# The last four experts' gate and up products: two parts of the tokens side by side, weight splits behind the sums, final-norm steps behind the product

## The chip, the cores and the metric

The kernel runs on one core of one Trainium2 chip. The metric is the device time of one execution in microseconds (us); the median over runs is what counts. The core's engines run side by side, each through a queue of its own in program order: TensorE (PE) does matrix products into the accumulation memory PSUM, ScalarE (ACT) and VectorE (DVE) work on elements, GpSimd (POOL) does small arithmetic and issues the indirect DMAs and some direct ones, SyncE (SP) issues the other DMAs. An instruction starts when its queue has reached it and all that it waits for has signalled.

## The reference

One encoder layer over 2048 tokens of width 1024. What the change touches is its last part, a mixture of 16 experts in which each expert picks its 256 tokens, and the norm at the very end:

```python
def expert_choice_moe(h, w_router, w_gate, w_up, w_down):
    ...
    gates, idx = lax.top_k(aff.swapaxes(1, 2), cap)
    xin = jax.vmap(lambda hb, ib: hb[ib])(h, idx)
    a = jnp.einsum("becd,edf->becf", xin, w_gate)
    b = jnp.einsum("becd,edf->becf", xin, w_up)
    y = jnp.einsum("becf,efd->becd", jax.nn.silu(a) * b, w_down)
    y = y * gates.astype(y.dtype)[..., None]
    out = jax.vmap(lambda ib, yb: jnp.zeros((S, D), yb.dtype).at[ib].add(yb))(
        idx.reshape(B, -1), y.reshape(B, -1, D))
    return out
...
    x = x + expert_choice_moe(rms_norm(x, g_ffn[l]), ...)
    return rms_norm(x, g_final)
```

All of it is float32. The kernel keeps that precision by splitting every operand into a high part, which TensorE takes exactly, and the rest: a = ah + al, and a product is ah·bh + ah·bl + al·bh.

## The kernel before, in words

`phase_moe` loops over the experts x = 0 to 15. An expert's 256 tokens lie transposed in `ht` (128 partitions, 8 blocks of the width, two parts, 256 tokens: part 0 the high one, part 1 the rest). Its weights are fetched in 12 jobs of 1 MB (job 12x + 2c + g: gate, g = 0, and up, g = 1, of the column blocks c = 0 to 3; then four jobs of the down matrix). `prep(i)` (L1721) splits job i: ACT copies the raw tile `wr` into `wh` (L1725), DVE subtracts to give `wl` (L1726), and then `fetch(i + 3)` puts the next load on SP's queue. Raw tiles have three buffers, split ones four.

For a column block c, PE multiplies the gate columns into PSUM tiles named `pa`, the up columns into tiles named `pb`, each in two halves j of 128 columns. Each of the names `pa`, `pb`, `py` and `tr` has two PSUM buffers that are taken in turn, so a new tile waits until the last but one of its name has been read.

Experts 0 to 11 and the last four (x at or above `LATE` = 12) do this in two ways:

- **Experts 0 to 11** (L1861 to L1866): for each half j a tile of its own holds two sums side by side. One product with 512 columns multiplies `wh` by both parts of the tokens (L1863), one with 256 columns multiplies `wl` by the high part (L1864). ACT copies the second sum out (L1865), DVE adds the first (L1866); after the gate's two halves ACT applies SiLU in place (L1869).
- **Experts 12 to 15** (L1856 to L1859): both halves in one tile, three products with 256 columns each (`mm3`, L45 to L47) that add up in PSUM. After both gate and up, ACT applies SiLU out of PSUM (L1883) and DVE multiplies by the up tile in PSUM (L1886).

Then `split` (L35) writes the product's high part `ah` (ACT, L37) and the rest `al` (DVE, L38). After the four blocks comes the down product (`mm3` again): two sums of 512 columns by two token halves, the first into `py`, the second into one `pa` and one `pb` tile. So an expert takes nine `pa` tiles in the first way (eight and one), five in the second (four and one).

In the last four experts the final norm is done alongside. `late_rows` gathers the residual rows of the expert's tokens; `late_piece` (L1774) adds the gated down product to them (L1777, DVE, reading PSUM; this is what sets the tile free), squares them on ACT (L1779) and multiplies by the norm's gain (L1780). All other rows are normed in sixteen blocks t of 128 rows by `final_step(n)` (L1791), which a fixed list `at` spreads over steps n = 12(x − 12) + job: `final_load(t)` at n = at[t] (POOL queue, L1742), `final_rows` two steps later (ACT squares, L1749, then a chain of 14 small POOL instructions, L1732, L55 and three times L67 to L70, that gives the reciprocal root), `final_scale` at +4 (DVE, L1755), `final_store` at +5 (SP, L1758). At its step 16 the rows of the expert before are normed (`late_norm`, L1788 and L1789), at 17 scattered to the output by two indirect DMAs (L1761). Before, even steps of the column blocks stand behind the gate's products, odd ones at the end of the block; in the down product there is one after each job.

Nothing reorders this: the schedule is manual, so the queues hold the instructions in the order in which the Python text issues them.

Of the kernel before, what the change touches and what calls it, by code (L numbers as in the profile page):

```python
# [10 lines left out]
F = mybir.dt.float32  # L11
# [4 lines left out]
AF = mybir.ActivationFunctionType  # L16
# [4 lines left out]
S, D, P = 2048, 1024, 128  # L21
# [22 lines left out]
def mm3(nc, ps, lh, ll, rh, rl, start, stop, **kw):  # L44
    nc.tensor.matmul(ps, lh, rh, start=start, stop=False, **kw)  # L45
    nc.tensor.matmul(ps, lh, rl, start=False, stop=False, **kw)  # L46
    nc.tensor.matmul(ps, ll, rh, start=False, stop=stop, **kw)  # L47
# [1586 lines left out]
def phase_moe(e):  # L1634


    nc, tc = e.nc, e.tc
    E, C = 16, 256
    LATE = E - 4
    with ExitStack() as ctx:  # L1640
# [194 lines left out]
        for x in range(E):  # L1835
# [8 lines left out]
            for c in range(4):  # L1844
                pp = []
                for g in range(2):
                    i = 12 * x + 2 * c + g
                    if c < 3 or g == 0:
                        prep(i + 3)
                    wh, wl = W.pop(i)  # L1850
                    s = gp.tile([P, 2, C], F, name=("si", "up")[g]) if x < LATE else None
                    if x >= LATE:
                        p = ps.tile([P, 2, C], F, name=("pa", "pb")[g])
                    for j in range(2):
                        js = slice(j * P, j * P + P)
                        if x >= LATE:  # L1856
                            for k in range(8):
                                mm3(nc, p[:, j], wh[:, k, js], wl[:, k, js], ht[:, k, 0], ht[:, k, 1], k == 0, k == 7)
                            continue  # L1859

                        p = ps.tile([P, 2, C], F, name=("pa", "pb")[g])  # L1861
                        for k in range(8):
                            nc.tensor.matmul(p, wh[:, k, js], ht[:, k], start=k == 0, stop=False, skip_group_check=True)  # L1863
                            nc.tensor.matmul(p[:, 0], wl[:, k, js], ht[:, k, 0], start=False, stop=k == 7, skip_group_check=True)  # L1864
                        nc.scalar.activation(s[:, j], p[:, 1], AF.Copy)  # L1865
                        nc.vector.tensor_add(s[:, j], s[:, j], p[:, 0])  # L1866
                    pp.append(s if x < LATE else p)
                    if g == 0 and x < LATE:
                        nc.scalar.activation(s, s, AF.Silu)  # L1869
                    if g == 0:  # L1870
                        final_step(i - 12 * LATE)
                if c == 0 and x + 1 < E:
                    lists(x + 1)
                if c == 1:
                    onehots(x + 2)
                    if x >= LATE:
                        late_rows(x)
                if c == 2 and x + 1 < E:
                    turn(x + 1, 0, 0)
                    turn(x + 1, 0, 1)  # L1880
                if x >= LATE:
                    s = gp.tile([P, 2, C], F, name="si")
                    nc.scalar.activation(s, pp[0], AF.Silu)  # L1883
                else:
                    s = pp[0]
                nc.vector.tensor_mul(s, s, pp[1])  # L1886
                split(nc, ah[:, 2 * c:2 * c + 2], al[:, 2 * c:2 * c + 2], s)
                if c == 3:
                    prep(12 * x + 10)
                elif c == 0 and x + 1 == E:  # L1890
                    fetch(len(jobs) - 1)
                final_step(12 * x + 2 * c + 1 - 12 * LATE)
            if x + 1 < E:
                ys = YS[x] = [gp.tile([P, D], F, name="y", bufs=2) for _ in range(2)]
            else:
# [215 lines left out]
```

## Time and profile before

| | us |
|---|---|
| median of three runs | 3091.11 (3089.67 to 3092.14) |
| the profiled execution, by its own time | 3091.91 |
| span of its records, first to last instruction | 3090.0 |
| mean granted TensorE clock over the span | 0.984 of full |
| PE busy | 2982.7 (97%) |
| DVE busy | 2034.8 (66%) |
| ACT busy | 1625.9 (53%) |
| POOL busy | 951.8 (31%) |

The last four experts run from 2797 us on. How to read it: an engine's busy share says little by itself; what counts is which engine is never idle in a stage, and what would make it wait. The timeline view lists an engine's instructions with the idle time ahead of each and the releaser in brackets; the windows view gives busy times, granted clock and DMA share of a stretch.

### The profile page before, as it was taken

The page shows a single profiled execution, that of the slowest core. Times are in us where ns is not written, and L with a number is a line of the kernel's source. Part 1 is how long each engine was busy: PE and PEld are TensorE (multiplying, and loading weights), DVE is VectorE, ACT ScalarE, POOL GpSimd, SP SyncE. Part 2 cuts the span into 40 slices and gives each one's busy share as a digit, 9 for nine tenths or more (in the row PEclk, how much of TensorE's full clock was granted, in tenths as well). Part 3 has the DMA queues.
Part 4 walks back from the last instruction along what each step waited for, and adds up shares of the span by engine and source line. Part 5 has one row for each costly group of instructions (what it writes and reads, how often), then busy time and mean ns, then how long its engine had stood idle before and what let it go on. Part 6 is the DMA issues. An engine that isn't in the chain of part 4 may idle for free.

```text
span 3090.0 us, 44235 instructions
## 1 busy us (share of the span) xinstructions
PE 2982.7 (97%) x16408; PEld 2501.3 (81%) x16409; DVE 2034.8 (66%) x3697; ACT 1625.9 (53%) x2744; POOL 951.8 (31%) x942
## 2 busy tenths in 40 slices
PE   7999999899999999999999998799999999999998
PEld 7997767677777777789788886588888888889998
DVE  5557878787878787665444445766666666666765
ACT  4444796576666667115433333455555555554544
POOL 1223568676845555101000001000000000003564
PEclk8999999999999999999999999899999999999999
DMA  5766163032121211456111112476777766668885
GB/s 190 223 207 186 40 190 80 17 77 65 32 77 48 65 42 52 147 198 204 46 55 62 63 55 97 146 218 204 219 220 213 224 216 205 205 205 259 300 297 208
DMA packets 314505, 452.35 MB, mean 146 GB/s; under 512 B 21185, under 2 KB 230337, under 8 KB 312946
## 3 DMA queue, kind: packets, MB, share of 16 engines
q1 hardware_dynamic: 282792, 373.08, 38.6%
q0 software_dynamic: 14928, 54.34, 6.1%
q10 hardware_dynamic: 16570, 22.11, 2.2%
q8 instruction: 129, 2.11, 0.3%
q14 instruction: 86, 0.70, 0.1%
HBM read 361.06 MB, written 88.28 MB: 145 GB/s over the span
## 4 chain that ended last, share of the span: by engine, by line
PE 87%; DVE 4%; ACT 2%; POOL 2%; DMA 2%; issue 2%; ACTq 0%; SPq 0%; POOLq 0%; DVEq 0%
PE po L922 7%; PE pa L1863 5%; PE pb L1863 5%; PE pst L889 3%; PE pmax L837 3%; PE pst L891 3%; PE pst L890 3%; PE pb L1864 3%; PE pa L1864 3%; PE po L924 2%; PE co L45 2%; PE co L47 2%; PE co L46 2%; PE pa L45 2%; PE pa L47 2%; PE pa L46 2%
## 5 line engine op out<-in xcount | busy, mean ns | idle before, releaser
L1726 DVE TENSOR_TENSOR wl<-wr,wh 128x2048 fp32r<-128x2048 f32 x191 | 436.2, 2291 | 285.0 <-ACT wh L1725 283.8
L894 ACT ACTIVATE ph<-pst 128x512 fp32r<-128x512 f32 x512 | 305.2, 596 | 232.8 <-PE pst L891 220.7
L906 DVE TENSOR_TENSOR pl<-pst,ph 128x512 fp32r<-128x512 f32 x512 | 351.2, 686 | 79.3 <-ACT pst L895 74.5
L838 DVE TENSOR_REDUCE mt<-pmax 128x1 f32<-128x512 f32 x496 | 338.6, 684 | 68.9 <-PE pmax L837 67.1
L1725 ACT ACTIVATE wh<-wr 128x2048 fp32r<-128x2048 f32 x191 | 362.2, 1905 | 36.2 <-PE pb L47 22.6
L895 ACT ACTIVATE pst<-pst 128x512 f32<-128x512 f32 x512 | 304.4, 595 | 0.0
L903 POOL TENSOR_SCALAR part<-ph,va 128x512 f32<-128x512 f32 x160 | 253.3, 1583 | 98.7 <-ACT ph L894 87.7
L1863 PE MATMUL pa<-ht,wh 128*128 128x512 f32 x768 | 274.5, 400 | 2.7 <-DVE si L1866 1.9
L1863 PE MATMUL pb<-ht,wh 128*128 128x512 f32 x768 | 272.2, 397 | 0.0
L1761 POOL DMA_INDIRECT x_s<-y,idx x24 | 46.3, 1929 | 717.1 <-ACT y L1924 621.1
L837 PE MATMUL pmax<-kh,q 96*128 96x512 f32 x496 | 200.6, 406 | 17.6 <-DVE mt L838 12.9
L1864 PE MATMUL pb<-ht,wl 128*128 128x256 f32 x768 | 215.5, 281 | 0.0
L1864 PE MATMUL pa<-ht,wl 128*128 128x256 f32 x768 | 215.5, 281 | 0.0
L905 POOL TENSOR_TENSOR acc<-acc,part 128x512 fp32r<-128x512 f32 x160 | 208.1, 1300 | 13.4
L889 PE MATMUL pst<-q,kl 96*128 96x512 f32 x512 | 207.3, 405 | 1.2 <-DVE pl L906 1.2
L922 PE MATMUL po<-ph,va 128*128 128x512 f32 x512 | 203.9, 398 | 0.0
L891 PE MATMUL pst<-q,kh 97*128 97x512 f32 x512 | 203.6, 398 | 0.2 <-ACT q L847 0.2
L922 PE MATMUL po<-pl,va 128*128 128x512 f32 x512 | 202.6, 396 | 0.1
L890 PE MATMUL pst<-q,kh 96*128 96x512 f32 x512 | 202.5, 396 | 0.0
L1863 PEld LDWEIGHTS pa<-ht,wh 128*128 128x128 f32 x768 | 144.2, 188 | 37.0 <-DVE si L1866 2.4
L1863 PEld LDWEIGHTS pb<-ht,wh 128*128 128x128 f32 x768 | 144.1, 188 | 34.9
L1864 PEld LDWEIGHTS pa<-ht,wl 128*128 128x128 f32 x768 | 145.1, 189 | 0.4
(659 smaller groups left out, 7971.5 us busy)
## 6 DMA issues: line engine op xcount, KB each, us to landing
wr<-in_w_exp_gate SPq DMA_DIRECT2D x64, 1024.0 KB
wr<-in_w_exp_up SPq DMA_DIRECT2D x64, 1024.0 KB
wr<-in_w_exp_down SPq DMA_DIRECT2D x63, 1024.0 KB
xr<-in_xT SPq DMA_DIRECT2D x16, 512.0 KB
wr<-in_x SPq DMA_DIRECT2D x16, 512.0 KB
k_s<-put SPq DMA_DIRECT2D x16, 512.0 KB
q<-q_s SPq DMA_DIRECT2D x32, 256.0 KB
wt<-in_xf SPq DMA_DIRECT2D x32, 256.0 KB
```

Of the source, the lines that this page charges most:

```text
L838: nc.vector.tensor_reduce(mt[:, t, j:j + 1], p, axis=AX.X, op=OP.max)
L889: nc.tensor.matmul(p, kl[:, ks], qh[0:96], start=True, stop=False)
L890: nc.tensor.matmul(p, kh[0:96, ks], ql, start=False, stop=False)
L891: nc.tensor.matmul(p, kh[:, ks], qh, start=False, stop=True)
L894: nc.scalar.activation(ph, p, AF.Exp, scale=scale)
L895: nc.scalar.activation(p, p, AF.Exp, scale=scale)
L906: return ph, pl, lambda: nc.vector.tensor_sub(pl, p, ph.bitcast(F))
L922: nc.tensor.matmul(OT[h, c], v[:, 0:128], t, start=kt == 0 and i == 0, stop=False, skip_group_check=True)
L1725: nc.scalar.activation(W[i][0], r, AF.Copy)
L1726: eng.tensor_sub(W[i][1], r, W[i][0].bitcast(F))
L1863: nc.tensor.matmul(p, wh[:, k, js], ht[:, k], start=k == 0, stop=False, skip_group_check=True)
L1864: nc.tensor.matmul(p[:, 0], wl[:, k, js], ht[:, k, 0], start=False, stop=k == 7, skip_group_check=True)
```

## The change

Experts 12 to 15 now make gate and up as the others do: two products for each block of the width instead of three, two tiles, ACT copies, DVE additions, SiLU in place. In them `prep(i + 3)` is called behind the two halves' sums (and the SiLU) instead of ahead of the products. And both final-norm steps of a column block are called at its end, behind the product, the split and, in block 3, `prep`; those in the down product stay where they were. The experts 0 to 11 are left as they are.

```diff
--- before.py
+++ after.py
@@ -1845,18 +1845,13 @@
                 pp = []
                 for g in range(2):
                     i = 12 * x + 2 * c + g
-                    if c < 3 or g == 0:
+                    more = c < 3 or g == 0
+                    if more and x < LATE:
                         prep(i + 3)
                     wh, wl = W.pop(i)
-                    s = gp.tile([P, 2, C], F, name=("si", "up")[g]) if x < LATE else None
-                    if x >= LATE:
-                        p = ps.tile([P, 2, C], F, name=("pa", "pb")[g])
+                    s = gp.tile([P, 2, C], F, name=("si", "up")[g])
                     for j in range(2):
                         js = slice(j * P, j * P + P)
-                        if x >= LATE:
-                            for k in range(8):
-                                mm3(nc, p[:, j], wh[:, k, js], wl[:, k, js], ht[:, k, 0], ht[:, k, 1], k == 0, k == 7)
-                            continue
 
                         p = ps.tile([P, 2, C], F, name=("pa", "pb")[g])
                         for k in range(8):
@@ -1864,10 +1859,13 @@
                             nc.tensor.matmul(p[:, 0], wl[:, k, js], ht[:, k, 0], start=False, stop=k == 7, skip_group_check=True)
                         nc.scalar.activation(s[:, j], p[:, 1], AF.Copy)
                         nc.vector.tensor_add(s[:, j], s[:, j], p[:, 0])
-                    pp.append(s if x < LATE else p)
+                    pp.append(s)
+                    if g == 0:
+                        nc.scalar.activation(s, s, AF.Silu)
+
+                    if more and x >= LATE:
+                        prep(i + 3)
                     if g == 0 and x < LATE:
-                        nc.scalar.activation(s, s, AF.Silu)
-                    if g == 0:
                         final_step(i - 12 * LATE)
                 if c == 0 and x + 1 < E:
                     lists(x + 1)
@@ -1878,18 +1876,15 @@
                 if c == 2 and x + 1 < E:
                     turn(x + 1, 0, 0)
                     turn(x + 1, 0, 1)
-                if x >= LATE:
-                    s = gp.tile([P, 2, C], F, name="si")
-                    nc.scalar.activation(s, pp[0], AF.Silu)
-                else:
-                    s = pp[0]
+                s = pp[0]
                 nc.vector.tensor_mul(s, s, pp[1])
                 split(nc, ah[:, 2 * c:2 * c + 2], al[:, 2 * c:2 * c + 2], s)
                 if c == 3:
                     prep(12 * x + 10)
                 elif c == 0 and x + 1 == E:
                     fetch(len(jobs) - 1)
-                final_step(12 * x + 2 * c + 1 - 12 * LATE)
+                for n in range(0 if x >= LATE else 1, 2):
+                    final_step(12 * x + 2 * c + n - 12 * LATE)
             if x + 1 < E:
                 ys = YS[x] = [gp.tile([P, D], F, name="y", bufs=2) for _ in range(2)]
             else:
```

On ACT, in expert 13 from the second block's end to the third's, before (`fs_...` is the sum of squares of one block of rows, here of t = 4 and at the end t = 5; `y` the late norm of expert 12; `ht` the next expert's tokens):

```order
L37 ACTIVATE ah<-si 128x512
L1725 ACTIVATE wh<-wr 128x2048
L1749 ACTIVATE fj,fs_28123<-fin 128x1024
L1789 ACTIVATE y<-y,ny_27749 128x512 x2
L1725 ACTIVATE wh<-wr 128x2048
L37 ACTIVATE ht<-tr 128x4x128 x2
L1883 ACTIVATE si<-pa 128x512
L37 ACTIVATE ah<-si 128x512
L1725 ACTIVATE wh<-wr 128x2048
L1749 ACTIVATE fj,fs_28281<-fin 128x1024
```

and now, from the start of the third block's sums to those of the fourth:

```order
L1860 ACTIVATE si<-pa 128x256 x2
L1864 ACTIVATE si<-si 128x512
L1725 ACTIVATE wh<-wr 128x2048
L1860 ACTIVATE up<-pb 128x256 x2
L1725 ACTIVATE wh<-wr 128x2048
L37 ACTIVATE ht<-tr 128x4x128 x2
L37 ACTIVATE ah<-si 128x512
L1749 ACTIVATE fj,fs_28051<-fin 128x1024
L1789 ACTIVATE y<-y,ny_27665 128x512 x2
L1860 ACTIVATE si<-pa 128x256 x2
```

The squares of t = 4 stood ahead of the third block's second weight split; they now stand behind the whole block, behind `ah`.

On DVE, in expert 13 from the fourth block's first split to the first piece of the down product, before (`fin` is the scaling of one block of rows, which waits for POOL's `ny`):

```order
L1726 TENSOR_TENSOR wl<-wr,wh 128x2048
L1755 SCALAR_TENSOR_TENSOR fin<-fin,ny_28128,gfin 128x1024
L1886 TENSOR_TENSOR si<-si,pb 128x512
L38 TENSOR_TENSOR al<-si,ah 128x512
L1726 TENSOR_TENSOR wl<-wr,wh 128x2048 x2
L38 TENSOR_TENSOR ht<-tr,ht 128x4x128
L1755 SCALAR_TENSOR_TENSOR fin<-fin,ny_28286,gfin 128x1024
L1726 TENSOR_TENSOR wl<-wr,wh 128x2048
L38 TENSOR_TENSOR ht<-tr,ht 128x4x128
L1777 SCALAR_TENSOR_TENSOR row<-py,gate,row 128x512
```

and now:

```order
L1861 TENSOR_TENSOR up<-up,pb 128x256 x2
L1880 TENSOR_TENSOR si<-si,up 128x512
L38 TENSOR_TENSOR al<-si,ah 128x512
L1726 TENSOR_TENSOR wl<-wr,wh 128x2048
L1755 SCALAR_TENSOR_TENSOR fin<-fin,ny_28056,gfin 128x1024
L1726 TENSOR_TENSOR wl<-wr,wh 128x2048
L38 TENSOR_TENSOR ht<-tr,ht 128x4x128
L1755 SCALAR_TENSOR_TENSOR fin<-fin,ny_28178,gfin 128x1024
L1726 TENSOR_TENSOR wl<-wr,wh 128x2048
L38 TENSOR_TENSOR ht<-tr,ht 128x4x128
L1777 SCALAR_TENSOR_TENSOR row<-py,gate,row 128x512
```

The scaling of t = 4 went from ahead of the block's product to between the two splits behind it; that of t = 5 stays, while its squares on ACT moved to the end of the block just before. POOL's queue keeps its order but for one exchange: `final_load` of t = 4 (and of 0, 8 and 13 in the other three experts) now stands behind the two gathers of `late_rows`.

## Rows read from the trace of the kernel before

**Rows 1.** Windows, expert 13: PE, PEld, DVE, ACT, POOL busy, clock, DMA share, GB/s

```profile
2868.00:2943.00 75.00, 75.00 (x554) 71.03 (x554) 52.59 (x68) 39.93 (x47) 46.05 (x95) 1.00 0.88 298
```

**Rows 2.** Timeline, PE: first products of a gate and an up block, early, late

```profile
2105.71 0.39 PE L1863 MATMUL pa<-ht,wh 128*128 128x512 f32 x1
...
2111.35 0.40 PE L1863 MATMUL pb<-ht,wh 128*128 128x512 f32 x1
...
2797.18 0.28 PE L45 MATMUL pa<-ht,wh 128*128 128x256 f32 x1
...
2802.93 0.28 PE L45 MATMUL pb<-ht,wh 128*128 128x256 f32 x1
```

**Rows 3.** Groups by line and form, ACT and DVE, 2450 to 2790 us (early experts)

```profile
L1865 ACT ACTIVATE up<-pb 128x256 f32<-128x256 f32 x40 | 14.4, 373 | 19.9 <-PE pb L1864 19.5
...
L1866 DVE TENSOR_TENSOR up<-up,pb 128x256 f32<-128x256 f32 x40 | 15.9, 417 | 5.5 <-ACT up L1865 4.8
...
L1886 DVE TENSOR_TENSOR si<-si,up 128x512 f32<-128x512 f32 x20 | 13.7, 687 | 0.2
...
L37 ACT ACTIVATE ah<-si 128x512 fp32r<-128x512 f32 x20 | 12.6, 632 | 48.5 <-DVE si L1886 48.5
```

**Rows 4.** Timeline, PE, expert 13: block 2's end, down's start, expert 14's start

```profile
2902.40 1.04 PE L1699 MATMUL tr<-ident,row 128*128 128x128 f32 x8
...
2914.79 0.40 PE L45 MATMUL py<-wh,ah 128*128 128x512 f32 x1
...
2937.52 0.28 PE L45 MATMUL pa<-ht,wh 128*128 128x256 f32 x1
```

**Rows 5.** Timeline, ACT, expert 13: squares of t = 4, a weight split

```profile
2898.98 1.06 ACT L1749 ACTIVATE fj<-fin 128x1024 bf16<-128x1024 f32 x1 [3.87 <-DMA fin<-x_s]
...
2901.27 1.90 ACT L1725 ACTIVATE wh<-wr 128x2048 fp32r<-128x2048 f32 x1
```

**Rows 6.** Timeline, POOL, expert 13: one root step, second scatter, load of t = 6

```profile
2903.21 2.32 POOL L68 TENSOR_TENSOR nr1t<-nr1t,ny 128x1 f32<-128x1 f32 x1
...
2912.90 1.21 POOL L1761 DMA_INDIRECT out<-y,idx  x1 [5.08 <-DVE wl L1726]
2914.11 0.59 POOL L1742 DMA_DIRECT2D fin<-x_s  x1
```

**Rows 7.** Timeline, DVE, expert 13

```profile
2889.35 2.81 DVE L1674 TENSOR_SCALAR oh<-iota,sl 128x128 bf16<-128x128 bf16 x16
...
2903.20 2.29 DVE L1726 TENSOR_TENSOR wl<-wr,wh 128x2048 fp32r<-128x2048 f32 x1 [4.97 <-ACT wh L1725]
...
2924.46 2.28 DVE L1726 TENSOR_TENSOR wl<-wr,wh 128x2048 fp32r<-128x2048 f32 x1
2927.44 0.69 DVE L38 TENSOR_TENSOR ht<-tr,ht 128x512 fp32r<-128x512 f32 x1 [0.69 <-ACT ht L37]
...
2938.44 0.74 DVE L1777 SCALAR_TENSOR_TENSOR row<-pa,gate,row 128x512 f32<-128x512 f32 x1
```

**Rows 8.** Source view of L1742, the sixteen loads of rows

```profile
DMA to landing us min/median/max: 6.6/8.7/9.9
```

**Rows 9.** Timeline, POOL, expert 12: root of t = 1 begins, load of t = 3

```profile
2838.97 1.25 POOL L1732 TENSOR_SCALAR nv<-fs 128x1 f32<-128x1 f32 x1 [5.39 <-ACT fj L1749]
...
2844.62 0.59 POOL L1742 DMA_DIRECT2D fin<-x_s  x1
```

**Rows 10.** Timelines, ACT and DVE, expert 15: squares of t = 13, scaling of t = 15, last piece

```profile
3038.83 1.04 ACT L1749 ACTIVATE fj<-fin 128x1024 bf16<-128x1024 f32 x1
...
3066.53 1.28 DVE L1755 SCALAR_TENSOR_TENSOR fin<-fin,ny,gfin 128x1024 f32<-128x1024 f32 x1 [2.26 <-POOL ny L70]
...
3077.01 0.48 DVE L1777 SCALAR_TENSOR_TENSOR row<-pb,gate,row 128x256 f32<-128x256 f32 x1 [1.19 <-PE pb L47]
```

**Rows 11.** Windows around an idle of PE in an early stage (columns as in rows 1)

```profile
596.30:604.30 8.00, 0.00 (x0) 0.00 (x0) 1.72 (x3) 2.36 (x5) 7.92 (x6) 0.66 0.02 5
604.40:609.10 4.70, 4.70 (x14) 4.02 (x15) 2.92 (x6) 1.68 (x4) 3.25 (x3) 0.50 0.02 3
```

## The prediction

> **What bounds the kernel now.** I read the windows of the last four experts first, then PE's waits, then PE's cadence, then the other queues around one expert's end. In the window of expert 13 PE is busy for all of its 75 us at a granted clock of 1.00, DVE for 52.6, ACT for 39.9, the DMA engines for 0.88 [rows 1]. PE's list of waits has nothing between 2500 us and the end. So PE's own issue rate bounds this stretch, and the change can win only by a faster cadence; it loses as soon as another queue lets PE wait.
>
> **Gain: the cadence.** A gate block's products take 2802.93 − 2797.18 = 5.75 us with three products of 256 columns, 2111.35 − 2105.71 = 5.64 with 512 and 256 [rows 2]. Gain 0.11 us a block, 8 blocks by 4 experts: **−3.5 us** (0.11%). A measurement of this kernel tells about 0.2% (6.2 us) from no change, so the gain alone would not be seen.
>
> **Cost of the sums.** Each expert gets 16 ACT copies of 0.37 and 16 DVE additions of 0.42 [rows 3], 6 us on ACT and 6.7 on DVE in some 70 us; DVE goes from 70% to about 80%. Both had idle time, so this costs PE nothing by itself. But the queues alternate and now hold more in a row. In block 1, in order: two copies 0.74, addition 0.42, SiLU as long as the copy `ah`, 0.63 [rows 3], `wh` 1.90 [rows 5], `wl` 2.29 [rows 7], two additions 0.83, `wl` 2.29, product 0.69, `ah` 0.63 [rows 3]: 10.4, and 2.81 of one-hots [rows 7]: 13.2 us, against 11.3 of PE. DVE enters block 2 about 1.9 us late. Block 3, with one split in its middle, gains some of it back.
>
> **Cost of the two smaller moves.** `prep` behind the sums starts one block of 5.6 us later; its split is needed three blocks, 17 us, after its products began, and takes 4.2, so it costs nothing while ACT and DVE are less than about 6 us late. Its load is issued as much later and awaited as much later: nothing. The exchange on POOL of `final_load` and the two gathers: nothing, ACT waited 3.87 us for that load [rows 5] and will now come for it later.
>
> **Cost of the moved final steps.** This is the large term. Expert 13, in the times of before:
>
> 1. The squares of t = 4 began at 2898.98 and were done, with their read-out, at 2900.1 [rows 5], 2.3 us ahead of block 2's last product (2902.40 [rows 4]). Now they stand behind its end: copy 0.37, `wh` 1.90, `wl` 2.29, two `ht` of 0.69, product 0.69, `ah` 0.63, squares 1.1: 8.4, so 2910.8; with the 1.9 us by which DVE is late, 2912.7.
> 2. On POOL the root of t = 4, two scatters and the load of t = 6 follow in that order. From 2900.1 to that load's issue, 2914.11, took 14.0 us; 5.08 of it the second scatter stood behind the first's landing [rows 6]. Now the issue is at 2924.8 to 2926.7.
> 3. The load lands 8.7 us after its issue [rows 8], 2933.5 to 2935.4. Behind it on ACT stand the squares of t = 6 (1.1) and the split of job 168, the next expert's first: `wh` 1.90, `wl` 2.29. It ends at 2938.8 to 2940.7, where it ended at 2926.74 [rows 7].
> 4. From there to the end of the last piece's read of the `pa` tile (2938.44 + 0.74 = 2939.18) the queues held 12.4 us: `ht`, two pieces, two more splits with their `wh`, a scaling. 0.69 of it was `ht` waiting for ACT [rows 7], so 11.8 remain: the tile is free at 2950.5 to 2952.5.
> 5. Expert 14's products start at 2937.52 [rows 4]. With two tiles to a block, their second half, 2.82 us later (2940.34), takes the buffer of that very tile; before, it was taken a whole block pair later, at some 2949. So PE waits **10.2 to 12.2 us**; I take 11.
>
> Expert 14 has the same rows 70 us later: 11 again. Expert 12 has no scatters: squares of t = 1 done 5.1 us after the down product starts (copy, addition, product, `ah`, `wh`, squares), the load of t = 3 issued 5.65 later [rows 9], landed after 8.7, squares 1.1, split 4.2, piece 0.74: 25.5 us, against 22.73 + 2.82 = 25.55 at which PE wants the tile. Nothing at the least, 2.7 with the lateness, 7 if POOL's root meets two weight splits (next part): I take 3.
>
> **The tail.** In expert 15 the squares of t = 13 go from 3.4 us ahead of block 2's end, as in expert 13, to 5.9 behind it, 9.3 later. From their end (3039.9) to the scaling of t = 15 (3066.53) POOL had two roots, two scatters and a third root, 26.6 us. The scaling moves to 3075.8; the last piece, 3077.01 with 1.19 of idle ahead [rows 10], moves 8.1 later. At the least each of the three roots loses the hold-up of the next part, 2.3, and 1 us is left. I take 4.
>
> **Two rules.** One step of POOL's root took 2.32 us, from 2903.21 on, beside a `wl` from 2903.20 that lasted 2.29 [rows 6, 7]; a whole root of 14 steps took 5.65 [rows 9]. The rows above hold one such hold-up per root; each further one costs 2.2. The Trainium skill says why (SBUF — State Buffer, "Who interferes with whom"): a DVE instruction with two inputs in SBUF and a GpSimd instruction that reads SBUF exclude each other for the whole instruction. By it the changed product, which read one input from PSUM and now reads both from SBUF, adds hold-ups of 0.69; the trace agrees for `wl`. The sum with two hold-ups a root is 2.2 us more for each expert's end.
>
> After an idle of 8 us PE ran at a granted clock of 0.50, 1.2 GHz, for the next 4.7 us [rows 11], which costs 2.3 us. Three waits of this kind cost up to 7; part of it falls where PE would have waited anyway: I take 2.5. The Trainium skill names this as what idle gaps between bursts do (TensorE: Matmul & The Clock Gate, "HAM oscillation — how this bites in real kernels"); rows 11 agree.
>
> **Sum.** −3.5 + 3 + 11 + 11 + 4 + 2.5 = **+28 us**. On the profiled execution (3091.91) that gives 3119.9; the median of the runs is 0.8 lower, so I forecast **3119 us**.
>
> **Rivals.**
>
> - *Everything stays covered* (not slower). Point of decision: in experts 13 and 14 the load of t = 6 (or 10) must go out by about 2915, as before, although its queue waits for squares that stand 10 us further back. It would need POOL's 14 us to shrink to 4. For it: the early experts run this very block, and PE's list of waits is empty from 2500 us on, through the last of them too. Against: they have no final steps. Time: −3.5, 3087.6. Chance 0.13.
> - *POOL goes faster when DVE waits.* A waiting DVE holds nothing up: the roots lose 2.3 each, and the second scatter's 5.08 may shrink. Expert ends 0, 7 and 7, tail 0, clock 1: +11.5, 3103. Chance 0.20.
> - *Lateness and hold-ups add.* 7 at expert 12, 15 at 13 and 14, tail 8, clock 7: +48, 3139. Chance 0.12.
> - *The edit does not do what it says*: the cadence stays 5.75 in the new place, or the tail gets shorter than I can see. Some us either way; 0.03.
>
> **How the numbers follow.** The forecast's own case has 0.52, and with its bounds (−3.5 + 0 + 10 + 10 + 1 + 0 = +17.5 to −3.5 + 7 + 12 + 12 + 4 + 5 = +36.5) runs from 3109 to 3128. With the second rival and the near side of the third the range that should hold 8 in 10 is 3095 to 3134; it leaves out the covered case and the far side of the third, some 0.2. Slower by over 0.2%: forecast, second and third rivals and a bit, 0.85. Within 0.2%: the covered case, 0.13. Faster: 0.02, since no row offers more than 3.5.
>
> **What would show it.** Right: PE's waits list `pa` behind the DVE piece (`row`, the line that is L1777 now) at three expert starts, two of them near 10 us; the load of t = 6 goes out 10 to 14 us later against the down product's start; gate blocks take 5.64. In the tail DVE's scaling of t = 15 waits for POOL, and the last piece comes after PE's end by more than now. Wrong: PE without idle through the last four experts, or waits that end on a weight split in the middle of an expert, which would make the moved `prep` the cause.

## The result, and the profile after

The changed kernel takes **3122.64 us** (median of 4 runs, 3120.95 to 3125.55) against 3091.62 for the kernel before on the same chip (4 runs): ratio **1.0101**, 95% interval 1.0089 to 1.0113, so 31 us slower, 28 to 35. The profiled execution has a span of 3123.8 us against 3090.0. Of these 33.8 us, 2.3 lie ahead of expert 12's first product (2797.18 [rows 2], now 2799.52), in stages that the change doesn't touch; 31.5 lie behind it.

PE's waits from 2500 us on, where the list of the kernel before was empty (us in total, times, longest):

```profile
PE pa L1858 <- DVE row L1777: 21.6, 3, 8.8
PE pa L1859 <- DVE wl L1726: 1.8, 1, 1.8
```

PE's timeline after the change: the first gate and up product of expert 12, the first product of expert 13 and the one that waited in it, the start of expert 13's down product, and the two later waits:

```profile
2799.52 0.39 PE L1858 MATMUL pa<-ht,wh 128*128 128x512 f32 x1
2805.16 0.40 PE L1858 MATMUL pb<-ht,wh 128*128 128x512 f32 x1
...
2868.65 0.39 PE L1858 MATMUL pa<-ht,wh 128*128 128x512 f32 x1
...
2877.44 0.80 PE L1858 MATMUL pa<-ht,wh 128*128 128x512 f32 x1 [5.83 <-DVE row L1777]
...
2923.34 0.39 PE L45 MATMUL py<-wh,ah 128*128 128x512 f32 x1
...
2956.15 0.79 PE L1858 MATMUL pa<-ht,wh 128*128 128x512 f32 x1 [6.92 <-DVE row L1777]
...
3038.69 0.80 PE L1858 MATMUL pa<-ht,wh 128*128 128x512 f32 x1 [8.81 <-DVE row L1777]
```

A gate block is 5.64 us, where it was 5.75 [rows 2]. Expert 12, which has no idle of its own, takes 69.13 us from first product to first product of the next (2868.65 − 2799.52), and 70.17 before: 1.04 gained. Then PE waits in the second half of the first gate block of each of the three experts that follow. Windows over expert 13's stretch and over the stretches at 0.50 (columns as in rows 1):

```profile
2868.00:2943.00 75.00, 69.17 (x374) 58.94 (x373) 51.01 (x73) 40.97 (x56) 36.01 (x76) 0.95 0.76 258
...
2875.80:2882.60 6.80, 5.16 (x16) 4.39 (x17) 4.36 (x9) 1.72 (x5) 4.77 (x13) 0.50 0.99 310
2954.30:2961.10 6.80, 4.95 (x15) 4.27 (x16) 4.57 (x9) 1.72 (x5) 4.96 (x13) 0.50 0.96 282
3032.80:3043.00 10.20, 4.31 (x13) 3.74 (x14) 8.61 (x11) 4.00 (x8) 7.83 (x15) 0.50 0.85 281
```

PE has 69.17 us of work in 75 us, and around the end of each wait and behind it it runs at a granted clock of 0.50, 1.2 GHz (the half clock, from here on). The whole account, in us:

| stretch | before | after | of it PE idle |
|---|---|---|---|
| expert 12 | 70.17 | 69.13 | 0 |
| expert 13 | 70.17 | 77.61 | 5.83 |
| expert 14 | 70.18 | 78.55 | 6.92 |
| expert 15 up to its down product | 46.07 | 58.33 | 1.83 + 8.81 |
| its down product | 23.20 | 23.94 | 0.46 |
| from PE's end to the end | 13.03 | 16.72 | |
| sum | 292.8 | 324.3 | 23.9 |

Experts 13 and 14, less expert 12's length and their idle, leave 2.65 and 2.50 us for the half clock; expert 15 some 2.5. So −4.2 (four times 1.04) + 23.9 + 7.6 + 3.7 = 31.0 of the 31.5.

What stands ahead of the late piece, expert 13. ACT's squares of t = 4, 5 and 6, and those of t = 10 in expert 14:

```profile
2920.10 1.04 ACT L1749 ACTIVATE fj<-fin 128x1024 bf16<-128x1024 f32 x1
...
2932.07 1.04 ACT L1749 ACTIVATE fj<-fin 128x1024 bf16<-128x1024 f32 x1
...
2937.33 1.06 ACT L1749 ACTIVATE fj<-fin 128x1024 bf16<-128x1024 f32 x1 [1.84 <-DMA fin<-x_s]
...
3021.71 1.06 ACT L1749 ACTIVATE fj<-fin 128x1024 bf16<-128x1024 f32 x1 [8.55 <-DMA fin<-x_s]
```

POOL: the root of t = 4 begins, the second scatter and the load of t = 6, the first and third step of the root of t = 5; then, in expert 14, the second scatter and the load of t = 10:

```profile
2921.33 0.44 POOL L1732 TENSOR_SCALAR nv<-fs 128x1 f32<-128x1 f32 x1 [20.22 <-ACT fj L1749]
...
2930.22 0.98 POOL L1761 DMA_INDIRECT out<-y,idx  x1 [3.18 <-DVE si L1880]
2931.20 0.59 POOL L1742 DMA_DIRECT2D fin<-x_s  x1
2933.30 1.25 POOL L1732 TENSOR_SCALAR nv<-fs 128x1 f32<-128x1 f32 x1 [1.51 <-ACT fj L1749]
...
2935.82 2.12 POOL L67 TENSOR_TENSOR nr1t<-nv,ny 128x1 f32<-128x1 f32 x1
...
3014.12 2.29 POOL L1761 DMA_INDIRECT out<-y,idx  x1 [7.21 <-DVE fin L1755]
3016.41 0.59 POOL L1742 DMA_DIRECT2D fin<-x_s  x1
```

DVE: in expert 12 the scaling of t = 1; in expert 13 the split beside that third step, the scaling of t = 5, the next expert's first split and the piece that PE waited for; in expert 14 the scaling and the split:

```profile
2862.25 1.28 DVE L1755 SCALAR_TENSOR_TENSOR fin<-fin,ny,gfin 128x1024 f32<-128x1024 f32 x1 [2.48 <-POOL ny L70]
...
2935.60 2.29 DVE L1726 TENSOR_TENSOR wl<-wr,wh 128x2048 fp32r<-128x2048 f32 x1
...
2940.97 1.28 DVE L1755 SCALAR_TENSOR_TENSOR fin<-fin,ny,gfin 128x1024 f32<-128x1024 f32 x1 [2.48 <-POOL ny L70]
2942.17 2.28 DVE L1726 TENSOR_TENSOR wl<-wr,wh 128x2048 fp32r<-128x2048 f32 x1
...
2955.35 0.74 DVE L1777 SCALAR_TENSOR_TENSOR row<-pa,gate,row 128x512 f32<-128x512 f32 x1
...
3020.84 1.28 DVE L1755 SCALAR_TENSOR_TENSOR fin<-fin,ny,gfin 128x1024 f32<-128x1024 f32 x1 [4.67 <-POOL ny L70]
...
3024.70 2.29 DVE L1726 TENSOR_TENSOR wl<-wr,wh 128x2048 fp32r<-128x2048 f32 x1 [2.58 <-ACT wh L1725]
```

Against the down product's start (2914.79 before [rows 4], 2923.34 now) that piece, the third of the expert's four, came at 23.7 us [rows 7] and comes at 32.0. PE wants its tile at 25.9 (2949.23). Two queues are late: ACT meets a load that has not landed, and DVE ahead of the very same split stands behind POOL's root.

In the tail, DVE's scaling of t = 15 and the last piece [rows 10]:

```profile
3101.64 1.28 DVE L1755 SCALAR_TENSOR_TENSOR fin<-fin,ny,gfin 128x1024 f32<-128x1024 f32 x1 [2.54 <-POOL ny L70]
...
3110.74 0.48 DVE L1777 SCALAR_TENSOR_TENSOR row<-pb,gate,row 128x256 f32<-128x256 f32 x1
```

Before, the last piece waited 1.19 us for PE; now it comes 3.7 us after PE's end (3107.08) and waits for nothing.

### The profile page after: what moved, and what is told of

The parts are those of the page before. It is cut to its first block, busy times and chain, and to the rows that moved or that the text cites. A ratio compares the mean times of both kernels' runs of the same rounds, so it can differ in the third digit from the quotient of the medians.

```text
span 3123.8 us, 43300 instructions
## 1 busy us (share of the span) xinstructions
PE 2987.3 (96%) x15897; PEld 2477.1 (79%) x15897; DVE 2057.5 (66%) x3761; ACT 1644.6 (53%) x2808; POOL 947.5 (30%) x942
## 5 line engine op out<-in xcount | busy, mean ns | idle before, releaser
L1858 PE MATMUL pa<-ht,wh 128*128 128x512 f32 x1024 | 374.0, 406 | 22.7 <-DVE row L1777 21.6
L1858 PE MATMUL pb<-ht,wh 128*128 128x512 f32 x1024 | 363.0, 397 | 0.0
L1859 PE MATMUL pa<-ht,wl 128*128 128x256 f32 x1024 | 290.9, 284 | 1.8 <-DVE wl L1726 1.8
L1859 PE MATMUL pb<-ht,wl 128*128 128x256 f32 x1024 | 287.4, 281 | 0.0
L1858 PEld LDWEIGHTS pa<-ht,wh 128*128 128x128 f32 x1024 | 196.1, 192 | 70.5 <-DVE row L1777 22.5
L1858 PEld LDWEIGHTS pb<-ht,wh 128*128 128x128 f32 x1024 | 192.3, 188 | 46.8
L1859 PEld LDWEIGHTS pa<-ht,wl 128*128 128x128 f32 x1024 | 197.5, 193 | 2.7 <-DVE wl L1726 2.1
```

## The experiments

Ratios are to runs of the kernel before on the same chip, with 95% intervals; microseconds from a ratio are worked out on 3091. Since the early stages differ by some us from run to run, I also give from each profile the time from expert 12's first product to the end (292.8 before, 324.3 after). "Tail" is the time from PE's end to the end. Diffs are against the changed kernel unless the text says otherwise.

**1. Which part costs what**

`steps_back`: only the final steps stand as before.

```diff
-                    if g == 0 and x < LATE:
+                    if g == 0:
                         final_step(i - 12 * LATE)
...
-                for n in range(0 if x >= LATE else 1, 2):
-                    final_step(12 * x + 2 * c + n - 12 * LATE)
+                final_step(12 * x + 2 * c + 1 - 12 * LATE)
```

> The changed kernel with one part undone: in the last four experts the even final step stands again behind each gate block's sums, the odd one alone at the block's end; side-by-side sums and the split behind them stay. The changed profile has 23.9 us of PE idle at expert ends (5.8, 6.9, 1.8 + 8.8, 0.5), three stretches at half clock and a tail 3.7 us longer. Theory (the moved final steps make the squares, the POOL roots and with them the down product's pieces late): nearly all of this goes, no `pa` wait above 2 us, cadence gain of 4.2 kept: 3086 to 3093. Rival (the sums and the later split by themselves fill ACT's and DVE's queues): at least half of the idle stays, 3103 or more.

Measured: 3108.24 us, ratio 1.0053 (1.0034 to 1.0072). The theory fell: 310.3 us from expert 12 on, so undoing the move gives back 14.0 of 31.5. The same waits are there, smaller, and the tail is 16.7 us as in the change:

```profile
PE pa L1858 <- DVE row L1777: 8.7, 3, 3.8
PE pa L46 <- DVE wl L1726: 1.3, 1, 1.3
```

`prep_front`: only the weight split stands as before.

```diff
-                    if more and x < LATE:
+                    if more:
                         prep(i + 3)
...
-                    if more and x >= LATE:
-                        prep(i + 3)
```

> The changed kernel with only the weight split put back ahead of the gate and up products; final steps stay at the block's end, sums stay side by side. Theory (the final steps are the cause, the moved split costs nothing): `pa` waits at the three expert ends stay at 5 to 11 us each, 3115 to 3125. Rival (the split behind the sums is what makes the queues late): the waits go, under 3100.

Measured: 3114.32 us, ratio 1.0080 (1.0059 to 1.0100); 318.1 us from expert 12 on. The waits stay, as the theory had it, but 6.2 us are given back, so the moved split is not free. Its list of waits:

```profile
PE pa L1858 <- DVE row L1777: 19.3, 3, 8.8
```

One place where they arise is seen on DVE at the end of expert 12. With the split in front it stands ahead of the gate block's sums, and the up block's sums come 1.2 us after the down product's start (2840.65 against 2839.46):

```profile
2836.72 2.29 DVE L1726 TENSOR_TENSOR wl<-wr,wh 128x2048 fp32r<-128x2048 f32 x1 [2.15 <-ACT wh L1725]
2838.93 0.75 DVE L1861 TENSOR_TENSOR si<-si,pa 128x256 f32<-128x256 f32 x2
2840.65 0.75 DVE L1861 TENSOR_TENSOR up<-up,pb 128x256 f32<-128x256 f32 x2 [0.97 <-ACT up L1860]
```

In the changed kernel it stands between the two, and they come 3.6 us after it (2849.51 against 2845.90):

```profile
2847.30 2.29 DVE L1726 TENSOR_TENSOR wl<-wr,wh 128x2048 fp32r<-128x2048 f32 x1 [2.50 <-ACT wh L1725]
2849.51 0.74 DVE L1861 TENSOR_TENSOR up<-up,pb 128x256 f32<-128x256 f32 x2
```

It is not so at every expert. The wait behind expert 12 is 3.41 us with the split in front and 5.83 in the change, but the one behind expert 13 is 8.75 against 6.92, since its third piece comes later (33.7 us after the down product's start against 32.0); behind expert 14 it is 7.12 against 8.81 and 1.83 more for weights.

`sums_only`: both edits above at once, so that of the change only the side-by-side sums are left.

> Only the side-by-side sums are kept; the split stands ahead of the products and the final steps where they stood in the kernel before. Theory: PE has the shorter cadence and no wait above 2 us in the last four experts, 3086 to 3091 (the gain of 4.2 us and at most a few us given back). Rival (nine `pa` tiles an expert rather than five are enough by themselves, because the down product's piece holds the next expert's buffer): PE waits at each of the three ends, 3 us or more each, 3097 to 3110.

Measured: 3102.02 us, ratio 1.0041 (1.0030 to 1.0052); 304.0 us from expert 12 on, 11.1 more than before. The theory fell here too. The time is in the rival's range, but less than half of the idle (3.9 of 8.6 us) is at the rival's tile: the up blocks wait for their own sums as well, and the tail is 2.7 us longer.

```profile
PE pb L1858 <- DVE up L1861: 4.7, 3, 1.8
PE pa L1858 <- DVE row L1777: 3.9, 3, 2.4
```

`steps_only`: the kernel before, with only its final steps moved.

```diff
-                    if g == 0:
+                    if g == 0 and x < LATE:
                         final_step(i - 12 * LATE)
...
-                final_step(12 * x + 2 * c + 1 - 12 * LATE)
+                for n in range(0 if x >= LATE else 1, 2):
+                    final_step(12 * x + 2 * c + n - 12 * LATE)
```

> The kernel before with only its final steps moved to the block's end in the last four experts; three products, five `pa` tiles an expert. Theory (lateness becomes a wait because the second half of the next expert's first gate block takes the buffer of the late piece): the pieces come 5 to 10 us later than in the kernel before, but the tile is wanted a whole block pair later, so PE's waits sum to under 5 us; with a tail 1 to 4 us longer, 3092 to 3100. Rival (late squares and splits stop PE without the tiles, through the weights): waits on weight splits or `pa` of 15 us and more in sum, 3107 or more.

Measured: 3104.34 us, ratio 1.0044 (1.0030 to 1.0058); 309.3 us from expert 12 on. Neither had it whole. The theory's point on the tile holds: the third piece comes at 26.4, 30.2 and 31.3 us after the down product's start (23.7, 23.7 and 25.2 before), and no product waits for it. But PE waits for a gather of the next expert's rows, which stands on POOL behind the late roots, and for weights, and the tail is 21.5 us, since the scaling of t = 15 waits 8.2 us for POOL:

```profile
PE tr L1699 <- DMA row<-h_s,idx: 2.2, 1, 2.2
PE pa L46 <- DVE wl L1726: 1.9, 1, 1.9
```

Together, from unrounded times: sums 11.1, the split behind them 6.4, the final steps 14.0 more. Added in this order they give the 31.5 by construction; that they nearly add up is shown by the other orders, in which the split costs 6.2 (between `prep_front` and the change) and the final steps 14.2 without the moved split and 16.5 without the sums either. Each of these is from one profiled execution (that of `sums_only` the shortest of its ten, that of `steps_only` the longest of its six). By the medians the three are 12.7, 3.7 and 14.8 us, so none of them is known to better than some 3 us. My theory that one of them was the cause was wrong.

**2. What makes the piece late, and how that reaches PE**

`down_tiles`: the down product's halves of columns exchange their tiles; other queues keep their order.

```diff
-name=("py", "pa")[n] if h == 0 else ("py", "pb")[n])
+name=(("py", "pa"), ("py", "pb"))[h][n] if x < LATE else (("pa", "py"), ("pb", "py"))[h][n])
```

> The changed kernel with only the names of the down product's tiles exchanged in the last four experts: its first half of columns sums into `pa` and `pb`, its second into the two `py`; what ACT, DVE and POOL do, and in which order, is the same. Theory (all lateness reaches PE through one place, the `pa` tile that the late second piece still holds when the next expert's first gate block wants it): the three waits of 5.8, 6.9 and 8.8 us go, and of the half-clock stretches behind them all or all but one; the late weight splits stay and let PE wait some 2 to 4 us before expert 15; the tail is still 3.7 us longer: +1 to +8 us on the kernel before, against +31 for the change. Rival (the tile is only the first thing that PE meets; the weights and the next expert's sums are as late): other waits take the place of these, +18 or more.

Measured: 3105.00 us, ratio 1.0045 (1.0030 to 1.0061), 310.2 from expert 12 on; between theory and rival. All three long waits are gone, but eight idles of 0.5 to 2.1 us (11.4 in sum) take their place. Four of them (6.0) stand where the down product now takes tiles that the late sums of the fourth block still hold; three are for weights (4.2), one is for the sums of a gate block (1.2). The first two kinds that the list shows:

```profile
PE pb L45 <- DVE up L1861: 4.1, 3, 2.1
PE pa L45 <- DVE si L1861: 2.0, 1, 2.0
```

`loads_early`:

```diff
-            for t in now(0):
+            for t in now(-2):
                 final_load(t)
```

> The changed kernel with each block's load for the final norm issued two steps earlier, so that it stands ahead of the previous block's POOL root and of the scatters. Theory on record (the late load of t = 6 and of t = 10 holds up ACT's squares and the split behind them): the ends of experts 13 and 14 lose 8 us or more each; +10 to +15 us on the kernel before. Rival (in experts 12 and 13 DVE's scaling, which waits 2.5 us for POOL's root, is what is late, and the load lies beside it): ends of experts 12 and 13 stay at 5 to 7 us, only expert 14's falls, by 3 to 5; +25 to +29.

Measured: 3117.46 us, ratio 1.0081 (1.0062 to 1.0101), +25: the rival. The idles are 5.8, 7.0 and 5.5 us. ACT waits for no load of rows any more, yet DVE's scaling in expert 13 waits as long as in the change, and the third piece comes at 32.1 us against 32.0:

```profile
2939.02 1.29 DVE L1755 SCALAR_TENSOR_TENSOR fin<-fin,ny,gfin 128x1024 f32<-128x1024 f32 x1 [2.48 <-POOL ny L70]
```

`scale_later`:

```diff
-            for t in now(5):
+            for t in now(6):
                 final_store(t)
...
-            for t in now(4):
+            for t in now(5):
                 final_scale(t)
```

> The changed kernel with each scaling (and its store) one step later, so that in the down product DVE meets it behind the first two pieces and doesn't wait there for POOL's root. Theory from the rows (DVE's wait for the root holds the next expert's first split at experts 12 and 13): their waits fall by 2 to 4 us each, expert 14's by little, since there the load is late: +20 to +26 on the kernel before. Rival (the scaling is hidden beside the load in every expert): waits within 1 us of those of the changed kernel, +29 to +33.

Measured: 3124.93 us, ratio 1.0100 (1.0080 to 1.0120): no gain, so this theory fell. DVE waits 1.7 us for a root in all (12.2 in the change), and the first piece of expert 13 comes 1.5 us earlier, at 20.1. But a split that no longer waits for the root now runs beside it and holds it up: in expert 12 the root of t = 1 takes 10.0 us (7.6 in the change), and the load behind it, of t = 3, goes out 18.6 us after the down product's start (16.3). ACT waits 21.3 us for loads of rows (10.4 in the change), and the third piece of expert 13 is at 32.2 again.

```profile
ACT fj L1749 <- DMA fin<-x_s: 21.3, 4, 12.2
```

`loads_and_scale`: both edits.

> Both: loads two steps earlier and scalings one step later. If load and root are two paths side by side that each alone keeps the pieces late, the two together give more than their sum: waits at expert ends 0 to 2, 0 to 4 and 0 to 4 us, at most one half-clock stretch, +3 to +12 on the kernel before. Rival (the longer row of sums and splits alone keeps the queues late): 10 us of waits or more remain, +16 or more.

Measured: 3100.54 us, ratio 1.0033 (1.0021 to 1.0045). One edit gave 6 us, the other none, the two together 21: from +31 to +10. So at experts 12 and 13 load and root are two paths that end nearly together, and each alone keeps the piece late. They are not independent: freeing DVE of its wait for the root made the load later. At expert 14 the load was the longer one (35.8 us with both late, 30.4 with the load early). What is left:

```profile
PE pa L1858 <- DVE row L1777: 6.4, 3, 2.7
PE pa L46 <- DVE wl L1726: 2.0, 1, 2.0
```

**3. Is there a version that wins?**

`all_early`: final steps back (the edit of `steps_back`), load and scaling as in the last run, and the last three blocks earlier. The diff is against the last run and leaves out the final steps.

```diff
-at = (2, 4, 6, 8, 14, 16, 18, 20, 26, 28, 30, 32, 34, 38, 39, 40)
+at = (2, 4, 6, 8, 14, 16, 18, 20, 26, 28, 30, 32, 34, 36, 37, 38)
...
-            for t in now(-2):
+            for t in [t for t in range(16) if max(at[t] - 2, 36 * (t > 12) + t // 15) == n]:
                 final_load(t)
```

> Side-by-side sums and the split behind them as in the change, the even final step back behind the gate block's sums, loads two steps earlier, scalings one step later, and the last three blocks' squares moved from steps 40 to 42 to steps 38 to 40 (scaled at 41 to 43, ahead of the last down product). Theory: the costs are separate and nearly add up (final steps 14, split 6, load and scaling together 21 of 31), so without them little is left: waits at the expert ends under 1 us each, the tail back within 1 us of the kernel before, and only the split's lateness before expert 15's down product (1 to 2 us, a half-clock stretch behind it): -2 to +4 us on the kernel before. Rival (sums and split by themselves leave 8 us of waits and more): +10 or more.

Measured: 3100.60 us, ratio 1.0029 (1.0018 to 1.0040). The tail is back at 13.0 us, so the late scaling of t = 15 was what made it longer. But the costs do not go one by one: 8.4 us of idle stay, as the rival had it, and +9 us in all.

```profile
PE pa L1858 <- DVE row L1777: 3.9, 2, 2.5
PE pb L1858 <- DVE up L1861: 2.7, 2, 2.3
PE pa L46 <- DVE wl L1726: 1.8, 1, 1.8
```

`front_in_block_3`, against `all_early`:

```diff
-                    if more and x < LATE:
+                    if more and (x < LATE or c == 3):
                         prep(i + 3)
...
-                    if more and x >= LATE:
+                    if more and x >= LATE and c < 3:
                         prep(i + 3)
```

> The same, but in the fourth block of each late expert the weight split stands ahead of the gate's products as in the kernel before. Theory (the split behind the sums costs 6 us because in the fourth block it bunches with the end of the expert; ahead of the products it is done while PE still has that block): 1 to 3 us below the run beside it, no wait above 1 us in the last four experts, -4 to +1 us on the kernel before. Rival (DVE then comes late to the up sums, as in the run with the sums alone, where PE waited 1.1 to 1.8 us three times for them): the same or slower than the run beside it.

Measured: 3100.20 us, ratio 1.0034 (1.0022 to 1.0046), no different from the run beside it: the rival. The wait for weights is gone, those for sums and pieces are not.

`tiles_and_front`, against the last one; the tiles are dealt by halves of the tokens, and `at` ends in 37, 37, 38 (loads, as in the run before, at 36, 36 and 37).

```diff
-name=("py", "pa")[n] if h == 0 else ("py", "pb")[n])
+name=(("py", "pa"), ("py", "pb"))[h][n] if x < LATE else ("py", ("pa", "pb")[n])[h])
```

> The run with the split in front in the fourth block (+10 on the kernel before), and the down product's tiles dealt by halves of the tokens: the first half sums into the two `py`, the second into `pa`, then into `pb`. The next expert's first gate block then takes a buffer that was read some 8 us before, and only its up block meets the late pieces, at a point 5.6 us later. The last blocks' squares stand one step later, so that ACT doesn't wait for their load. Theory (what is left of the cost is the late piece meeting the gate block's tile, 2.0, 2.6 and 0.7 us, one wait for up sums of 2.7, and the half-clock stretches behind them): no wait above 1 us in the last four experts, no half-clock stretch in them, -5 to 0 us on the kernel before. Rival (DVE is short of time with the sums, and the lateness only moves on to the next place): 5 us of waits or more stay, +5 or more.

Measured: 3091.25 us against 3088.64, ratio 1.0015 (1.0006 to 1.0024). The third piece comes at 27.0, 29.1 and 26.4 us, as late as in the two runs before or later, and PE doesn't meet it. No stretch at half clock is left, but some 3.4 us of idle are, so the time misses the theory's range, by less than the rival had it. The longest of them:

```profile
PE pb L1858 <- DVE up L1861: 1.6, 1, 1.6
```

The gain of the cadence is eaten up, and the kernel before is still a little faster.

`change_with_tiles`: the changed kernel with this deal of the tiles alone.

> The changed kernel (+31 on the kernel before) with only the down product's tiles dealt by halves of the tokens, as in the run before this one; split, final steps, loads and scalings as in the change. The pieces are as late as in the change. Theory (the lateness costs what it costs because of the tile that it meets): the next expert meets the late piece in its up block's second half, 5.6 us later, and that piece is read 1.4 us later, so each `pa` wait of 5.8, 6.9 and 8.8 us becomes a `pb` wait 4.2 us shorter: 1.6, 2.7, 4.6 (and 1.8 for the weights of expert 15 as before); two half-clock stretches rather than three; tail still 3.7 longer: +14 to +20. Rival (the tile hardly matters, DVE's row of work is what PE waits for wherever it meets it): +25 or more.

Measured: 3108.24 us, ratio 1.0052 (1.0038 to 1.0066), +16. The three waits are 1.57, 2.65 and 2.65 us, with 0.95 and 1.61 for weights ahead of the last and 1.93 for weights in the last down product. The pieces are as late as in the change (30.8, 33.9 and 34.9 us); half of the cost was the tile in which PE meets them.

```profile
PE pb L1858 <- DVE row L1777: 6.9, 3, 2.6
```

All runs side by side, by their profiles (PE idle: the sum of idles above 0.3 us; third piece: us after the down product's start, in experts 12, 13, 14):

| kernel | ratio | expert 12 to the end | PE idle | tail | third piece |
|---|---|---|---|---|---|
| before | 1 | 292.8 | 0 | 13.0 | 23.7, 23.7, 25.2 |
| sums only | 1.0041 | 304.0 | 8.6 | 15.7 | 25.6, 27.3, 25.8 |
| steps only | 1.0044 | 309.3 | 4.1 | 21.5 | 26.4, 30.2, 31.3 |
| steps back | 1.0053 | 310.3 | 10.5 | 16.7 | 28.0, 29.9, 26.7 |
| split in front | 1.0080 | 318.1 | 19.3 | 16.6 | 28.3, 33.7, 32.0 |
| the change | 1.0101 | 324.3 | 23.9 | 16.7 | 30.7, 32.0, 35.8 |
| down tiles | 1.0045 | 310.2 | 11.4 | 16.7 | 30.8, 32.1, 36.4 |
| loads early | 1.0081 | 318.8 | 18.7 | 16.7 | 30.7, 32.1, 30.4 |
| scaling later | 1.0100 | 325.8 | 24.7 | 16.7 | 31.3, 32.2, 38.5 |
| loads and scaling | 1.0033 | 305.7 | 9.4 | 16.6 | 26.4, 28.5, 27.1 |
| all early | 1.0029 | 302.9 | 8.4 | 13.0 | 26.3, 27.5, 24.9 |
| front in block 3 | 1.0034 | 302.3 | 8.4 | 13.1 | 27.0, 28.3, 25.7 |
| tiles and front | 1.0015 | 295.2 | 3.4 | 13.1 | 27.0, 29.1, 26.4 |
| change with tiles | 1.0052 | 310.3 | 12.6 | 15.9 | 30.8, 33.9, 34.9 |

## Why the prediction was right, and where it was not

**The direction, the size and the place were right.** 3122.6 lies 3.6 us above the forecast of 3119, and inside the range. PE waits at the three expert starts that were named, in the second half of the gate block, for the piece on `pa`. Of the signs named, the load of t = 6 fell short: against the down product's start it goes out 8.5 us later (from −0.7 to 7.9), where 10 to 14 were named; that of t = 10 in expert 14 goes out 13.2 later. The chain's end holds in numbers: from the first split's end (2942.17 + 2.28 = 2944.45) to the piece's end (2955.35 + 0.74 = 2956.09) it is 11.6 us, 11.8 forecast in step 4. That the buffer is what turns lateness into idle (step 5) is shown by `steps_only`, where pieces 2.7 to 6.5 us later let no product wait for them, and by the two runs that change only the tiles.

**Term by term**, forecast and measured: gain −3.5 and −4.2; end of expert 12, 3 and 5.8; of 13, 11 and 6.9; of 14, 11 and 10.6; tail 4 and 3.7; clock 2.5 and 7.6. The waits sum to 25 and 23.4, which is luck: expert 12's came out 2.8 us above its term and expert 13's 4.1 below, and 1.8 of expert 14's are for weights, which the sum didn't have.

- *Step 1* holds. The squares of t = 4 are done 9.9 us after block 2's last product (2921.24 − 2911.37); 8.4 to 10.3 were forecast.
- *Step 2 was over-sized.* From there to the load's issue it is 10.0 us (2931.20), not 14.0 [rows 5, 6]: the root took 4.0 us, with no split beside it, and the second scatter waited 3.18 us, not 5.08. This is the second rival's mechanism, at that one place. The next root, beside the splits, took 7.6 us (2933.30 to 2940.93) with steps of 1.25, 1.11 and 2.12 us. The rule of the Trainium skill (SBUF — State Buffer, "Who interferes with whom"), that a DVE instruction with two inputs in SBUF and a GpSimd one that reads SBUF exclude each other, agrees with both.
- *Step 3 named the wrong last arrival.* It let the split wait for the load alone. The load did land late (ACT took it 6.1 us after its issue in expert 13, 8.7 forecast), but DVE's scaling, waiting for POOL's root, came out behind it in expert 13 and alone in expert 12; in expert 14 it was the load. `loads_early` shows that at experts 12 and 13 the load by itself decides nothing, `scale_later` that DVE's wait for the root by itself decides nothing either. In expert 12 this is also part of why 5.8 stands for 3: the scaling of t = 1 waits 2.5 us for a root that took some 7.6, the hold-up that I had listed as the bound of 7. Its squares were late as well, done 8.6 us after the down product's start instead of 5.1.
- *"This costs PE nothing by itself"*, of the sums, **failed**: alone they cost 11 us here. The argument was busy shares, 80% of DVE. Shares say nothing of a row that stands still for others: the copy waits for PE, the addition for the copy, SiLU for the addition, a split for ACT. What the profile of `sums_only` shows is where PE meets it: 4.7 us at up blocks whose own sums are late, 3.9 at the piece's tile. That the hand-overs make them late, rather than the additions' own time, no run here separates.
- *"Nothing"*, of the moved `prep`, **failed**: 6 us. I asked only when its weights are needed, with a slack of 6 us. That slack was used up: the change waits 1.83 and 0.46 us for weight splits, `prep_front` for none. The rest I put down to what stands behind it: 4.2 us of split between the two sums of the last block, shown above at the end of expert 12.
- *The tail* had the right size and the right waiter, but more than one cause: the moved steps alone make it 8.5 us longer (21.5, near the 8.1 of the forecast's upper case), yet it is also nearly as long with the final steps back (16.7) and with the sums alone (15.7). The scaling of t = 15 is late in all of them, and in all of them, as in the change, the last piece starts 9.1 us after it.
- *The clock* was mis-sized: each of three waits costs some 2.5 us, none of it hidden. These 5 us too few are why the time lies above the forecast.

So the forecast had the mechanism and the sum, and put 25 us of waits on the moved final steps, which are 14 of the 31.5. The sums and the split use up the same slack: with nine tiles to an expert the piece, read for 0.7 us, could come 25.9 − 23.7 − 0.7 = 1.5 us later than before, no more.

## What to carry to other kernels

Before a wait is priced, look at where the late result is met: count how many tiles of each name a unit of work takes. Here five became nine, the next expert's first block met the late tile, and a new deal of three names took half of the cost away. Where two queues hand work to each other, a change that "has idle time to use" should be checked by the queue's last result against the moment it is wanted (23.7 against 25.9 us here), not by busy shares. And when two paths end nearly together, taking away one can show nothing; try both at once before a path is acquitted.

## What the runs showed of the hardware that was not expected

The price of an idle of PE is not set by its length alone. Windows in `sums_only`, behind an idle of 2.37 us in a gate block, and behind one of 1.81 us ahead of an up block:

```profile
2937.20:2943.90 6.70, 6.67 (x30) 5.77 (x31) 5.04 (x9) 3.90 (x7) 3.38 (x10) 0.77 0.97 323
...
2903.40:2910.40 7.00, 7.00 (x38) 6.03 (x39) 5.19 (x7) 2.98 (x4) 1.25 (x2) 1.00 0.65 227
```

In `steps_only`, behind an idle of 1.94 us in expert 15's down product:

```profile
3064.40:3071.20 6.80, 6.79 (x44) 6.79 (x45) 4.91 (x5) 5.28 (x5) 5.66 (x14) 0.75 0.00 0
```

And in `loads_and_scale`, behind one of 1.95 us at the same place:

```profile
3061.60:3068.40 6.80, 6.78 (x56) 6.78 (x57) 4.96 (x6) 5.28 (x5) 2.62 (x8) 1.00 0.19 77
```

A mean of 0.77 or 0.75 over these 6.7 or 6.8 us costs 1.5 to 1.7 us (a quarter of the stretch or a little less), nearly as much as the idle itself, and two idles of the same length at the same place differ. In `steps_back` an idle of 3.79 us is followed by a mean of 0.54 over 6.8 us, which costs 3.1, no less than the idles of 5.8 to 8.8 us in the change did. I had taken 2.5 us for all waits together, from one idle of 8 us [rows 11]. The Trainium skill tells of PE falling back to its half clock behind the waits between bursts of products (TensorE: Matmul & The Clock Gate, "HAM oscillation — how this bites in real kernels"). The traces agree behind the idles of 5.83 to 8.81 us (0.50) and show it behind some of about 2 us, but not behind those of 1.81 and 1.95 us; what decides it for the short ones stays open.

Also open are some 0.5 and 0.7 us in experts 13 and 14 of `tiles_and_front` that no idle over 0.3 us accounts for, and whether the sums would pay with fewer instructions on DVE at the ends of the experts, which was not tried.
